# Roots by one activation function, thirteen warm products and earlier LayerNorm steps in a one-core decoder layer

## The chip, the cores and the metric

The kernel runs on one core of one Trainium2 chip. The metric is the device time in microseconds (us) of one launch, the median over the runs. Before the change it is 1084.68 us (three runs, 1083.5 to 1085.56).

## The reference

One layer of a decoder with two groups of heads, on 256 prompt tokens and 8 x 4 sample tokens, 288 columns in all, float32. D_MODEL is 2048, the convolution and pool groups have 1024 channels each, the feed-forward part 8192.

```python
def rmsnorm(x, g):
    return x * lax.rsqrt(jnp.mean(x * x, axis=-1, keepdims=True) + EPS) * g

h = rmsnorm(x, norm1_g)
proj = h @ w_in + b_in
a, gate, z = proj[..., :1024], proj[..., 1024:2048], proj[..., 2048:]
u_ext = concat([hist_conv, a * sigmoid(gate)])
c = silu(layernorm(depthwise_causal_conv(u_ext, conv_w, conv_b), ln_g, ln_b))
z_ext = concat([hist_pool, z])
d = multiscale_pool(z_ext, pos0)            # windows 2, 4, 8, 16
p = group_matmul(d, pool_w) * pool_scale
x = x + concat([c, p]) @ w_out
h2 = rmsnorm(x, norm2_g)
x = x + square(relu(h2 @ w_ff1)) @ w_ff2
y = rmsnorm(x, norm_f)
```

Outputs are y for both groups of tokens and the new histories (the last 30 inputs of the convolution, the last 15 of the pools).

## The kernel before

**Layout.** Channels lie on the 128 partitions and the 288 tokens in the free dimension. A product is a 128x128 block of weights against 128x288 columns, summed in PSUM. To keep float32 precision with fp32r operands, each operand is split into a high part (`hi`, a cast) and a low part (`lo`, the rest), and each product is made of three: hi x hi, lo x hi and hi x lo. In the profile `whi` and `wlo` are weights; `hx`, `dx`, `mx`, `ax` and `fx` are the right-hand sides of w_in, the pools and their part of w_out, the convolution's part of w_out, w_ff1 and w_ff2.

**Stages.** w_in's column pairs come in the order of SEQUENCE: convolution pairs c0 to c7, pools p3 to p0, and the pools' own products P3 to P0. Then w_out runs over the pools' rows (eight groups `g` of two banks, `mixp`), and again over the convolution's rows (`mixc`), while LayerNorm over the convolution's output is done between the products of the first pass. Then come four chunks of w_ff1 and w_ff2, the final norm and the output.

**First products.** x and the first weights come pair by pair of rows, k = 0, 2, ..., 14 (`first_load`). `first_split` (L359) makes their parts: `hi` on ScalarE (L364, L371), the right-hand sides on ScalarE (L369) and for k = 0 on VectorE (L367), the low parts on VectorE (L373, L376). Ahead of them TensorE runs warm products that nothing reads (L213). The first gemm has four banks (pairs c0 and c1) and 24 products for each pair of rows.

**Norms.** The products run on the columns before their norm is known; what comes out is multiplied by the row of inverse roots afterwards. `squares` (L411) sums x squared: ScalarE squares (L418), VectorE adds (L420); a copy from the high weights of k = 4 (L413) holds the squares back until those are there. `rsqrt_sums` (L238) sums over the partitions by products of one column (TensorE), has ScalarE take the square root (L250), then VectorE the reciprocal and a Newton step (L253 to L256). `spread` (L259) brings the result to all partitions by three products with an identity. It serves the first norm (`first_sums`, `first_rows`) and LayerNorm (`ln_sums`, `ln_rows`). The second norm (L638) and the final one (L704 to L712) use ScalarE's Sqrt and `inverse_root` (L231). `load_table` (L207) applies a function to one column, so that its ACT_TABLE_LOAD comes early.

**Order.** A scheduler orders each engine's instructions by readiness and priority; a lower number goes first, and priorities go by the order of the code. `later(by)` (L111) adds `by` to it, a million as a rule; a negative value brings what it encloses ahead of everything else that is ready. `issue_after(ins)` holds an instruction behind another. `chain` keeps TensorE's products in the order of the code until it is cleared ahead of P1. `between` (L338) has a gemm call a step at a given row pair: LayerNorm's mean, sums and rows come in groups 5, 6 and 7 of the first w_out pass (L579). `classes` (L332) puts the first products of a gemm in another order; TURN (L70) has 48 places. Normally the right-hand side alternates between rows 1 and 3 and rows 0 and 2 of its tile.

**Low parts.** WAYS (L73) tells by stage who makes the low part of a block: V is VectorE (L279), G is GpSimd (L282), D is the negated high part by ScalarE (L276) and a DMA from GpSimd's queue that adds the weights to it (L277). There are six raw blocks and five split ones. GpSimd also makes the products of the convolution's history (L464), which wait for `u_all` (L449).

Of the kernel before, what the change touches and what calls it, by code (L numbers as in the profile page):

```python
# [9 lines left out]
F32 = mybir.dt.float32  # L10
# [76 lines left out]
def trunk_kernel(ctx: ExitStack, tc: tile.TileContext, io):  # L87
# [119 lines left out]
    def load_table(func, src):  # L207

        return nc.scalar.activation(few[: src.shape[0], :], src, func)

    load_table(AF.Sqrt, ones[:, 0:1])
    warm = ms("warm")
    for j in range(9):  # L213
        nc.tensor.matmul(warm[:, 0, 0:P], ones, ones, start=True, stop=True)
# [16 lines left out]
    def inverse_root(mean, root, y, out):  # L231

        nc.vector.reciprocal(y, root)
        nc.vector.scalar_tensor_tensor(out=root, in0=mean, scalar=EPS, in1=y, op0=ALU.add, op1=ALU.mult)
        nc.vector.scalar_tensor_tensor(out=root, in0=root, scalar=-0.5, in1=y, op0=ALU.mult, op1=ALU.mult)
        nc.vector.scalar_tensor_tensor(out=out, in0=root, scalar=1.5, in1=y, op0=ALU.add, op1=ALU.mult)

    def rsqrt_sums(parts, scale, after=None):  # L238

        pq = ms("pt")
        pt = pq[:, 0, :]
        for n, t in enumerate(parts):
            for j in range(3):
                last = mm(pt[:TB, j : j + 1], t[:, j * TB : (j + 1) * TB], ones[:, 0:1], start=n + j == 0, stop=n == len(parts) - 1 and j == 2)
        st = const.tile([TB, 12], F32, name=nm("st"))
        s = [st[:, 3 * j : 3 * j + 3] for j in range(4)]
        nc.vector.tensor_scalar(s[0], pt[:TB, 0:3], scale * DC, EPS, op0=ALU.mult, op1=ALU.add)
        nc.scalar.activation(s[1], s[0], AF.Sqrt)  # L250
        if after is not None:
            load_table(after, s[1][:, 0:1])
        nc.vector.reciprocal(s[2], s[1])  # L253
        nc.vector.tensor_tensor(s[3], s[2], s[2], op=ALU.mult)
        nc.vector.scalar_tensor_tensor(out=s[3], in0=s[3], scalar=-0.5, in1=s[0], op0=ALU.mult, op1=ALU.mult)
        nc.vector.scalar_tensor_tensor(out=s[2], in0=s[3], scalar=1.5, in1=s[2], op0=ALU.add, op1=ALU.mult)  # L256
        return s[2], pq[:, 1, :T], last
# [101 lines left out]
    def first_split(k0):  # L359
# [5 lines left out]
        for k in range(k0, k0 + 2):  # L365
            if k == 0:
                nc.vector.tensor_scalar(hx[k][0], xT[:, k, :], v("norm1_g", k), None, op0=ALU.mult)  # L367
# [4 lines left out]
        for b in blocks:  # L372
            nc.vector.tensor_tensor(lo[:, b], raw[:, b], f32(hi[:, b]), op=ALU.subtract)  # L373
# [66 lines left out]
    def conv_pair(i, banks):  # L440
        up = u_all[:, i, 0:UO]
        us = samples(u_all[:, i, UO:UL], US)
        ta, gate = [b[:, :T] for b in banks]
        for b in (gate, ta):
            nc.vector.tensor_tensor(b, b, rb, op=ALU.mult)
        tg = tmpp.tile([P, 2, T], F32, name=nm("tg"), tag="ag", bufs=2)[:, 0, :]
        nc.scalar.activation(tg, gate, AF.Sigmoid, bias=v("b_in", 8 + i))
        for out, a, b in ((up[:, CH:UO], ta[:, :SEQ], tg[:, :SEQ]), (us[:, :, CH:US], samples(ta[:, SEQ:T], NS), samples(tg[:, SEQ:T], NS))):
            nc.vector.scalar_tensor_tensor(out=out, in0=a, scalar=v("b_in", i), in1=b, op0=ALU.add, op1=ALU.mult)  # L449
# [74 lines left out]
    def first_sums():  # L524
        diag.append(rsqrt_sums(squares(), 1.0 / D, AF.Sigmoid))
        return diag[0][2]

    def first_rows():
        pr, last = spread(diag[0])
        nc.scalar.copy(rb, pr)  # L530
# [17 lines left out]
    load_table(AF.Sqrt, f32(mixp[1][0])[:, 0:1])  # L548
# [12 lines left out]
    def ln_sums():  # L561
        ssc = None
        for c in cs:
            nc.vector.tensor_tensor(c, c, norm["mean"][:, None, :].to_broadcast([P, 2, T]), op=ALU.subtract)
# [219 lines left out]
```

## Time and profile before

| | us |
|---|---|
| median of three runs | 1084.68 |
| lowest, highest | 1083.5, 1085.56 |
| the profiled execution | 1084.57 |
| its span, first to last instruction | 1082.8 |
| TensorE busy, of the span | 1071.5 |
| VectorE, ScalarE, GpSimd busy | 635.4, 479.0, 173.6 |
| mean granted TensorE clock | 0.997 of full |

A row of the timeline has start and duration in us, the engine (PE is TensorE's products, PEld its loading of weights, DVE VectorE, ACT ScalarE, POOL GpSimd), the source line, the operation, what is written and read (buffer numbers left out), the shapes and the count of instructions merged in the row. In brackets stands how long the engine was idle before it, and what ended the idle time. A row of the stage windows has the window's borders, its length, and for each engine the busy time and the count; where one engine is asked for, it stands alone, followed by the granted clock, the share of the DMA engines and GB/s. A row of the DMA view ends with the time from issue to landing. Busy times of products overlap, since each begins while the one before drains; the distance of two starts is the step of the stream. A float32 product that is not fp32r counts as two instructions.

### The profile page before, as it was taken

The numbers are of one execution on the slowest core, as the hardware profiler recorded it, in microseconds if no ns is written. First come the engines' busy times: TensorE is split into PE (matmuls) and PEld (weight loads), VectorE is DVE, ScalarE is ACT, GpSimd is POOL, SyncE is SP. The second block draws the span as 40 slices with busy tenths as digits, with TensorE's granted clock in tenths as the row PEclk, the third lists the DMA queues.
The fourth block names the chain that finished last, engine by engine and source line by source line (L and its number), as shares of the span: only waits on it lengthen the run. The fifth ranks groups of instructions, "written<-read, shape, count | busy, mean of one in ns | idle before, by whom it ended". The sixth has DMA issues, their size and how long they took to land.

```text
span 1082.8 us, 19572 instructions
## 1 busy us (share of the span) xinstructions
PE 1071.5 (99%) x8198; PEld 1069.9 (99%) x8198; DVE 635.4 (59%) x818; ACT 479.0 (44%) x585; POOL 173.6 (16%) x180
## 2 busy tenths in 40 slices
PE   9999999999999999999999999999999999999996
PEld 9999999999999999999999999999999999999996
DVE  8899999678655544445544444545544445554553
ACT  8654445475544433334443333444433334444441
POOL 0878979512000000000000000000000000000001
PEclk9999999999999999999999999999999999999998
DMA  9896468545555555555555555555555555555522
GB/s 325 281 273 185 137 196 239 176 152 177 173 164 170 172 166 169 174 164 169 171 168 168 175 165 169 174 167 167 174 165 168 174 169 165 173 166 168 173 78 88
DMA packets 58296, 190.71 MB, mean 176 GB/s; under 512 B 6240, under 2 KB 11232, under 8 KB 58208
## 3 DMA queue, kind: packets, MB, share of 16 engines
q1 hardware_dynamic: 56336, 184.35, 53.9%
q0 software_dynamic: 1008, 3.67, 1.9%
q8 instruction: 64, 1.05, 0.4%
q10 hardware_dynamic: 864, 1.44, 0.4%
q14 instruction: 24, 0.20, 0.1%
HBM read 185.16 MB, written 4.28 MB: 175 GB/s over the span
## 4 chain that ended last, share of the span: by engine, by line
PE 77%; issue 20%; ACT 1%; DVE 0%; DMA 0%; POOL 0%; POOLq 0%
PE ac L305 77%; PE pp L305 1%; DMA wr<-in_w 0%; ACT whi L274 0%; POOL xT L720 0%; ACT n L595 0%; DVE wlo L279 0%; PE pt L305 0%; PE pmean L305 0%; POOLq L770 0%; DVE xT L695 0%; DVE n L592 0%; ACT whi L364 0%; ACT mx L597 0%; DVE hx L367 0%
## 5 line engine op out<-in xcount | busy, mean ns | idle before, releaser
L274 ACT CAST whi<-wr 128x1024 fp32r<-128x1024 f32 (+1 forms) x332 | 348.0, 1049 | 551.4 <-PE ac L305 533.5
L279 DVE TENSOR_TENSOR wlo<-wr,whi 128x1024 fp32r<-128x1024 f32 x288 | 353.1, 1226 | 348.5 <-ACT whi L274 348.5
L305 PE MATMUL ac<-ax,whi 128*128 128x288 f32 x2048 | 351.0, 292 | 0.0
L305 PE MATMUL ac<-fx,whi 128*128 128x288 f32 x2048 | 350.2, 292 | 0.0
L305 PEld LDWEIGHTS ac<-ax,whi 128*128 128x128 f32 x2048 | 296.0, 187 | 0.0
L305 PEld LDWEIGHTS ac<-fx,whi 128*128 128x128 f32 x2048 | 295.6, 187 | 0.0
L305 PE MATMUL ac<-ax,wlo 128*128 128x288 f32 x1024 | 217.4, 292 | 0.0
L305 PE MATMUL ac<-fx,wlo 128*128 128x288 f32 x1024 | 216.4, 292 | 0.0
L305 PEld LDWEIGHTS ac<-ax,wlo 128*128 128x128 f32 x1024 | 162.6, 187 | 0.0
L305 PEld LDWEIGHTS ac<-fx,wlo 128*128 128x128 f32 x1024 | 162.3, 187 | 0.0
L305 PE MATMUL ac<-hx,whi 128*128 128x288 f32 x768 | 131.8, 295 | 1.2 <-DVE hx L367 1.2
L720 POOL TENSOR_TENSOR xT<-xT,rf 128x288 f32<-128x288 f32 x4 | 3.1, 795 | 800.1 <-ACT rf L724 800.1
L305 PEld LDWEIGHTS ac<-hx,whi 128*128 128x128 f32 x768 | 112.1, 190 | 1.4 <-ACT hx L369 1.4
L282 POOL TENSOR_TENSOR wlo<-wr,whi 128x512 fp32r<-128x512 f32 x74 | 100.3, 1410 | 35.3 <-ACT whi L274 34.3
L461 DVE SCALAR_TENSOR_TENSOR pc<-u_all,vec,pc 128x256 f32<-128x256 f32 x232 | 99.5, 483 | 1.9 <-ACT pc L458 0.7
L305 PE MATMUL ac<-hx,wlo 128*128 128x288 f32 x384 | 80.1, 294 | 0.0
L305 PEld LDWEIGHTS ac<-hx,wlo 128*128 128x128 f32 x384 | 61.1, 190 | 0.0
L305 PE MATMUL ac<-dx,whi 128*128 128x288 f32 x256 | 46.0, 296 | 0.0
L305 PE MATMUL ac<-mx,whi 128*128 128x288 f32 x256 | 45.1, 294 | 0.1
L664 DVE SCALAR_TENSOR_TENSOR t<-ac,r 128x576 f32<-128x576 f32 x32 | 24.2, 758 | 25.1 <-PE ac L305 25.1
L305 PEld LDWEIGHTS ac<-dx,whi 128*128 128x128 f32 x256 | 38.0, 188 | 0.2
L305 PEld LDWEIGHTS ac<-mx,whi 128*128 128x128 f32 x256 | 37.5, 188 | 0.6 <-ACT mx L597 0.4
(133 smaller groups left out, 533.6 us busy)
## 6 DMA issues: line engine op xcount, KB each, us to landing
wr<-in_w SPq DMA_DIRECT2D x335, 512.0 KB, 3.8
wlo<-in_w POOLq DMA_DIRECT2D x7, 512.0 KB, 7.7
xT<-in_xT SPq DMA_DIRECT2D x8, 288.0 KB, 7.3
wr<-in_w SPq DMA_DIRECT2D x5, 256.0 KB, 3.6
out_u_out<-u_all SPq DMA_DIRECT2D x1, 1208.0 KB, 9.3
u_all<-in_hist_c SPq DMA_DIRECT2D x8, 136.0 KB, 6.2
out_z_out<-z_all SPq DMA_DIRECT2D x1, 668.0 KB, 9.9
z_all<-in_hist_p SPq DMA_DIRECT2D x4, 152.0 KB, 7.5
```

Source lines behind the costliest of these rows:

```text
L274: nc.scalar.copy(hi, raw)
L279: nc.vector.tensor_tensor(lo, raw, f32(hi), op=ALU.subtract)
L282: nc.gpsimd.tensor_tensor(lo[:, j : j + 2, :], raw[:, j : j + 2, :], f32(hi[:, j : j + 2, :]), op=ALU.subtract)
L305: last = nc.tensor.matmul(*args, **kw)
L461: nc.vector.scalar_tensor_tensor(out=dst, in0=up[:, w : w + SEQ], scalar=cwv[:, w : w + 1], in1=pc, op0=ALU.mult, op1=ALU.add)
L664: nc.vector.scalar_tensor_tensor(out=t, in0=bk[:, :, :T], scalar=0.0, in1=both(rows2[0]), op0=ALU.max, op1=ALU.mult)
L720: eng.tensor_tensor(xk, xk, r[:, None, :].to_broadcast([P, n, T]), op=ALU.mult)
```

## The change

- All four roots use ScalarE's `Abs_reciprocal_sqrt`, which reads the sums in PSUM and adds EPS as its bias. The reciprocal on VectorE is gone, and for the first norm and LayerNorm the operation that scaled the sums too: the scale is in the column that sums them. The Newton step stays, with its intermediate in PSUM. The tables are loaded ahead at the same places.
- 13 warm products for 9.
- In `first_split` the low parts of the first weights are held behind the first right-hand side on VectorE.
- The first norm's steps (squares, sums, rows and the copy `rb`), the gating of the pairs c0 and c1 in `conv_pair` and LayerNorm's sums and rows get a priority ahead of everything else.
- LayerNorm's mean, sums and rows are called one row pair sooner, 12 products each.
- In both passes of w_out the order TURN is in the second group and not the third.
- In making `mixc`, Silu of a pair is held behind the copy of the pair before.

```diff
-        return nc.scalar.activation(few[: src.shape[0], :], src, func)
-    load_table(AF.Sqrt, ones[:, 0:1])
+        return nc.scalar.activation(few[: src.shape[0], :], src, func, bias=ones[: src.shape[0], 0:1], scale=0.0)
+    load_table(AF.Abs_reciprocal_sqrt, ones[:, 0:1])
     warm = ms("warm")
-    for j in range(9):
+    for j in range(13):
...
-    def inverse_root(mean, root, y, out):
-        nc.vector.reciprocal(y, root)
-        nc.vector.scalar_tensor_tensor(out=root, in0=mean, scalar=EPS, in1=y, op0=ALU.add, op1=ALU.mult)
-        nc.vector.scalar_tensor_tensor(out=root, in0=root, scalar=-0.5, in1=y, op0=ALU.mult, op1=ALU.mult)
-        nc.vector.scalar_tensor_tensor(out=out, in0=root, scalar=1.5, in1=y, op0=ALU.add, op1=ALU.mult)
+    def inverse_root(mean, y, t, out, after=None):
+        nc.scalar.activation(y, mean, AF.Abs_reciprocal_sqrt, bias=eps[: y.shape[0], :])
+        if after is not None:
+            load_table(after, y[:, 0:1])
+        nc.vector.scalar_tensor_tensor(out=t, in0=mean, scalar=EPS, in1=y, op0=ALU.add, op1=ALU.mult)
+        nc.vector.scalar_tensor_tensor(out=t, in0=t, scalar=-0.5, in1=y, op0=ALU.mult, op1=ALU.mult)
+        nc.vector.scalar_tensor_tensor(out=out, in0=t, scalar=1.5, in1=y, op0=ALU.add, op1=ALU.mult)
...
-    def rsqrt_sums(parts, scale, after=None):
+    def rsqrt_sums(parts, column, after=None):
         pq = ms("pt")
-        pt = pq[:, 0, :]
+        mean, t = pq[:TB, 0, 0:3], pq[:TB, 0, 4:7]
...
-        s = [st[:, 3 * j : 3 * j + 3] for j in range(4)]
-        nc.vector.tensor_scalar(s[0], pt[:TB, 0:3], scale * DC, EPS, op0=ALU.mult, op1=ALU.add)
-        nc.scalar.activation(s[1], s[0], AF.Sqrt)
...
-        return s[2], pq[:, 1, :T], last
+        inverse_root(mean, st[:, 0:3], t, st[:, 4:7], after=after)
+        return st[:, 4:7], pq[:, 1, :T], last
...
-                nc.vector.tensor_scalar(hx[k][0], xT[:, k, :], v("norm1_g", k), None, op0=ALU.mult)
+                first = nc.vector.tensor_scalar(hx[k][0], xT[:, k, :], v("norm1_g", k), None, op0=ALU.mult)
...
         for b in blocks:
-            nc.vector.tensor_tensor(lo[:, b], raw[:, b], f32(hi[:, b]), op=ALU.subtract)
+            with tc.issue_after(first.ins) if k0 == 0 else nullcontext():
+                nc.vector.tensor_tensor(lo[:, b], raw[:, b], f32(hi[:, b]), op=ALU.subtract)
...
     def conv_pair(i, banks):
+        with later(-LATER if i < 2 else 0):
...
     def first_sums():
-        diag.append(rsqrt_sums(squares(), 1.0 / D, AF.Sigmoid))
+        with later(-LATER):
+            diag.append(rsqrt_sums(squares(), mean_d, AF.Sigmoid))
...
     def first_rows():
-        pr, last = spread(diag[0])
-        nc.scalar.copy(rb, pr)
+        with later(-LATER):
+            pr, last = spread(diag[0])
+            nc.scalar.copy(rb, pr)
...
     def ln_sums():
+        with later(-LATER):
...
     def ln_rows():
-        norm["rows"], last = spread(norm["sums"])
+        with later(-LATER):
+            norm["rows"], last = spread(norm["sums"])
...
-    BETWEEN = {5: {4: ln_mean}, 6: {6: ln_sums}, 7: {2: ln_rows}}
+    BETWEEN = {5: {2: ln_mean}, 6: {4: ln_sums}, 7: {0: ln_rows}}
...
-            last = gemm(each(bk), [mixp[k] for k in korder], between=BETWEEN.get(g, {}), classes=TURN if g == 2 else "")
+            last = gemm(each(bk), [mixp[k] for k in korder], between=BETWEEN.get(g, {}), classes=TURN if g == 1 else "")
...
-            nc.scalar.activation(n[:, m, :], n[:, m, :], AF.Silu, bias=v("ln_b", i), scale=v("ln_g", i))
+            with tc.issue_after(copied) if j else nullcontext():
+                nc.scalar.activation(n[:, m, :], n[:, m, :], AF.Silu, bias=v("ln_b", i), scale=v("ln_g", i))
...
-        nc.scalar.copy(mh, n)
+        copied = nc.scalar.copy(mh, n).ins
...
-        last = gemm(each(bk), mixc, classes=TURN if g == 2 else "")
+        last = gemm(each(bk), mixc, classes=TURN if g == 1 else "")
...
-        nc.scalar.activation(root, mean, AF.Sqrt, bias=eps)
-        inverse_root(mean, root, r2, r2)
+        inverse_root(mean, r2, root, r2)
...
-    nc.scalar.activation(root, sums_f, AF.Sqrt, bias=eps[:TB, :])
-    inverse_root(sums_f, root, first, s_f)
+    s_f = cst[:TB, 6:9]
+    inverse_root(sums_f, cst[:TB, 2:5], ends[:TB, 0, 4:7], s_f)
```

More of the change, by code (lines that the diff above doesn't have):

```diff
@@ L547, in trunk_kernel @@
             pool_products(i)
-    load_table(AF.Sqrt, f32(mixp[1][0])[:, 0:1])
+    load_table(AF.Abs_reciprocal_sqrt, f32(mixp[1][0])[:, 0:1])
     with later(2 * LATER):
@@ L706, in trunk_kernel @@
                 nc.tensor.matmul(idle[:, 0:P], ones, ones, start=True, stop=True)
-    root, first, s_f = [cst[:TB, 2 + 3 * j : 5 + 3 * j] for j in range(3)]
-    nc.scalar.activation(root, sums_f, AF.Sqrt, bias=eps[:TB, :])
-    inverse_root(sums_f, root, first, s_f)
+    s_f = cst[:TB, 6:9]
+    inverse_root(sums_f, cst[:TB, 2:5], ends[:TB, 0, 4:7], s_f)
     for spread_f in (rows_f, again):
```

46 lines of the change are left out of this document (20 added, 26 removed).

## The prediction

> **What bounds the kernel now.** The page first: its first part tells which engine fills the span.
>
> ```profile
> span 1082.8 us, 19572 instructions
> PE 1071.5 (99%) x8198; PEld 1069.9 (99%) x8198; DVE 635.4 (59%) x818; ACT 479.0 (44%) x585; POOL 173.6 (16%) x180
> ```
>
> TensorE is in work 99% of the span, so only three things can move the end: time in which it waits, time in which it steps slowly, and the ends of the span where it has nothing to do. A busy share doesn't show slow steps, so I next read starts of products in the timeline, and one row of the stage windows.
>
> ```profile
> 191.26 0.42 PE L305 MATMUL ac<-dx,wlo 128*128 128x288 f32 x2
> ...
> 192.04 0.42 PE L305 MATMUL ac<-dx,wlo 128*128 128x288 f32 x2
> ...
> 204.78 0.43 PE L305 MATMUL ac<-dx,wlo 128*128 128x288 f32 x2
> ...
> 205.58 0.43 PE L305 MATMUL ac<-dx,wlo 128*128 128x288 f32 x2
> ```
>
> ```profile
> 284.00:1069.00 785.00, 785.00 (x6040) 1.00 0.52 163
> ```
>
> From one low-part pair to the next are six products: 0.78 us in the first two rows (130 ns a product), 0.80 us in the next two (133.3 ns). The row of the windows, TensorE alone, has 6040 products in 785.00 us, 130.0 ns each: the long stage runs on the quick step. The slow step comes up after a break in the stream and stays until the products that TURN has put in another order have passed: in the first w_out pass TURN is at g == 2, and there 0.80 becomes 0.78.
>
> Then the start, where the first real product waits and a second, larger loss stands.
>
> ```profile
> 1.04 4.21 PE L214 MATMUL warm<-ones 128*128 128x128 f32 x18 [1.04 <-DVE cst L229]
> ...
> 5.59 0.54 ACT L369 ACTIVATE hx<-xT,vec 128x288 fp32r<-128x288 f32 x1 [0.35 <-DMA xT<-in_xT]
> ...
> 5.89 0.36 DVE L367 TENSOR_SCALAR hx<-xT,vec 128x288 fp32r<-128x288 f32 x1
> ...
> 6.40 1.30 PE L305 MATMUL ac<-hx,whi 128*128 128x288 f32 x4 [1.15 <-DVE hx L367]
> ...
> 8.45 2.12 PE L305 MATMUL ac<-hx,whi 128*128 128x288 f32 x8
> ...
> 10.84 1.05 ACT L364 CAST whi<-wr 128x1024 fp32r<-128x1024 f32 x1
> ...
> 11.80 0.96 ACT L369 ACTIVATE hx<-xT,vec 128x288 fp32r<-128x288 f32 x2
> ...
> 12.67 0.20 ACT L413 COPY z_all<-whi 128x10 f32<-128x10 f32 x1
> 12.89 2.41 ACT L418 ACTIVATE z_all<-xT 128x576 f32<-128x576 f32 x4
> ...
> 15.21 1.04 ACT L364 CAST whi<-wr 128x1024 fp32r<-128x1024 f32 x1
> ...
> 16.59 1.22 DVE L373 TENSOR_TENSOR wlo<-wr,whi 128x1024 fp32r<-128x1024 f32 x1
> ...
> 16.83 2.27 PE L305 MATMUL ac<-hx,whi 128*128 128x288 f32 x16
> ...
> 18.94 1.21 PE L305 MATMUL ac<-hx,wlo 128*128 128x288 f32 x8
> ```
>
> The nine warm products (18 instructions) end at 5.25; TensorE idles 1.15 us and starts the real work at 6.40 with products 240 ns apart (eight last 2.12 us at 8.45, against 1.21 us at 18.94). About 18 run so before the clock is granted near 10.6: 18 x 110 ns = 2.0 us lost.
>
> **The change, part by part.** The sum is made against the profiled execution: 1084.57 us, its span 1082.8 and 1.8 around it; the median of the runs is 1084.68, so the two may stand for each other.
>
> *Warm products, and the norm's first product ahead of the low parts.* Thirteen are 26 instructions. The grant came 4.2 us after unbroken work began (6.40 to 10.6); unbroken from 1.04 it comes near 5.2, when some 19 have run (0.21 us each); the last 7 at half that end near 6.0. With L367 ahead of L373 on VectorE, L367 can start with L369 at 5.59 and the first product near 6.13, where hx of k = 1 is ready: 0.27 us sooner, and at full step. The low part behind it comes near 6.65, as the fifth product asks for it.
>
> [...]
>
> Without waits this would be worth 0.27 + 2.0 = 2.3 us. But the squares (L413, L418) now have a million steps of priority, and ScalarE does them as soon as the cast that gates them is done at 11.89 (10.84 + 1.05). Ahead of hx and the cast of rows k = 6, 7 then stand 0.20 + 2.41: hx ends at 11.89 + 2.61 + 0.96 = 15.46, the cast at 16.50, the low part (1.22) at 17.75. TensorE, with 72 products of three pairs at 130 ns, is there at 6.13 + 9.4 = 15.5 and waits about 1.0 us. Before, it used this cast at 16.83 + 8 x 0.13 = 17.87 (I take the first 8 of those 16 as the pair before) and the low part at 18.94. So 1.2 us is left; I take 1.15. Later pairs cost ScalarE 2.7 us each (a square 0.6, hx 0.96, cast 1.04), TensorE 3.1: no further wait. The wait falls on the 73rd product, inside the first TURN (the 37th to the 84th): should that leave the slow step until the next one, some 126 products later, 0.4 is lost. Bounds: 0.4 (that, or a square's addition and a leftover of hx ahead of the low part), 2.3 if the squares don't come first.
>
> *Roots.* The two steps over three columns (first norm, LayerNorm) go from five VectorE operations to three, the other two from four to three; ScalarE reads PSUM itself.
>
> ```profile
> 32.47 0.59 PE L305 MATMUL pt<-ones,z_all 128*96 128x1 f32 x6
> ...
> 33.28 0.21 ACT L250 ACTIVATE st<-st 96x3 f32<-96x3 f32 x1 [1.44 <-DVE st L249]
> ...
> 35.52 0.16 DVE L256 SCALAR_TENSOR_TENSOR st<-st 96x3 f32<-96x3 f32 x1
> 35.74 0.74 PEld L305 LDWEIGHTS pt<-ident,st 96*128 96x128 f32 x6 [0.17 <-DVE st L256]
> ...
> 1071.27 0.26 ACT L708 ACTIVATE cst<-ends,cst 96x3 f32<-96x3 f32 x1 [0.19 <-PE ends L703]
> 1071.57 0.17 DVE L233 RECIPROCAL cst<-cst 96x3 f32<-96x3 f32 x1 [1.53 <-ACT cst L708]
> 1071.85 0.16 DVE L234 SCALAR_TENSOR_TENSOR cst<-ends,cst 96x3 f32<-96x3 f32 x1
> ...
> 1072.45 0.91 PE L712 MATMUL ends<-ident,cst 96*128 96x96 f32 x6 [0.21 <-DVE cst L236]
> ```
>
> First norm: from 33.06 to 35.68 the step took 2.6 us; one ScalarE operation (0.26 at L708) and three of 0.16 with their gaps make some 1.1, so the 0.17 us that the spread product waited goes: I take 0.1. Tail: everything from 1071.27 to 1072.45 sets the end, and L233 leaves with the gap behind it (1071.57 to 1071.85): 0.25 us, 0.1 to 0.3 should the PSUM target of the next three cost. The second norm's reciprocal is hidden under a running stream. ACT_TABLE_LOADs: as many as before, if the new function's table holds Square and Copy as Sqrt's does; the trace can't show that.
>
> *LayerNorm 12 products sooner.* All three steps and what they issue (4 + 6 + 6 TensorE instructions, VectorE's and ScalarE's; no DMA) move together, 12 x 0.133 = 1.6 us.
>
> ```profile
> 195.80 0.48 DVE L461 SCALAR_TENSOR_TENSOR c<-u_all,vec,pc 128x256 f32<-128x256 f32 x1
> ...
> 201.15 0.65 PE L305 MATMUL pmean<-sum_c,ones 128*128 128x288 f32 x2
> ...
> 208.94 0.46 DVE L571 TENSOR_TENSOR q<-q 128x288 f32<-128x288 f32 x1
> ...
> 210.11 0.59 PE L305 MATMUL pt<-ones,q 128*96 128x1 f32 x6
> ...
> 219.00 0.43 PE L305 MATMUL ac<-dx,whi 128*128 128x288 f32 x2
> ...
> 219.55 0.54 PE L305 MATMUL ac<-mx,whi 128*128 128x288 f32 x2
> ...
> 221.59 0.42 PE L305 MATMUL ac<-mx,wlo 128*128 128x288 f32 x2
> ```
>
> The mean's input is done at 196.28, 4.9 us ahead of its use: moving by 1.6, and TensorE's own 1.2 at the start, leaves 2. The sums end 0.7 us ahead of 210.11, with equal distance to the mean as before, and with priority. At the far end 14 products start between 219.00 and 221.59, 2.59 us where 1.87 are due: 0.72 us of waiting for mx, which 1.6 us more room covers. The new order of Silu and copy gives the first pair of mx sooner still. I take 0.72; bounds 0 and 0.8.
>
> *TURN one group sooner, twice.* 48 products each at 130 instead of 133.3: 2 x 0.16 = 0.32; bounds 0 and 0.4.
>
> *Priorities for the first two convolution pairs.* Nothing for TensorE by themselves; they decide the first rival.
>
> Sum: 1.15 + 0.1 + 0.25 + 0.72 + 0.32 = 2.54; **1084.57 - 2.54 = 1082.0 us.**
>
> **Rivals.** *(1) A low part by DMA gives the start's gain back.* In convolution 3 GpSimd issues an accumulating DMA behind two products of the history.
>
> ```profile
> 40.56 4.33 POOL L464 TENSOR_TENSOR prd<-u_all,vec 128x992 f32<-128x992 f32 x2 [0.94 <-DVE u_all L449]
> ...
> 44.83 1.06 POOL L277 DMA_DIRECT2D wlo<-in_w  x1
> ...
> 50.91 0.42 PE L305 MATMUL ac<-hx,wlo 128*128 128x288 f32 x2
> ```
>
> ```profile
> wlo<-in_w POOLq DMA_DIRECT2D x1, 512.0 KB, 5.8
> ```
>
> By the DMA view's row of that issue it lands at 44.83 + 5.8 = 50.6, and TensorE wants it at 50.91: 0.3 us to spare. TensorE 1.25 us sooner waits 0.95 unless the issue moves. The priorities speak for a move (u_all is ready some 2 us sooner, L464 starts in GpSimd's idle 0.94); a static order that puts L464 elsewhere speaks against. With the wait comes the slow step up to TURN at i == 5, some 250 x 3.3 ns = 0.8: 1082.0 + 1.8 = 1083.8.
>
> *(2) The squares don't delay the cast:* 2.3 in place of 1.15: 1080.9.
>
> *(3) The w_out groups are interleaved again.* Now the first group's sum (L609) comes 12.3 us behind the first mx product at 219.55, the time of two groups.
>
> ```profile
> 231.87 0.76 DVE L609 TENSOR_TENSOR xT<-xT,ac 128x576 f32<-128x576 f32 x1 [2.40 <-PE ac L305]
> ```
>
> Then TURN, now in the second, is scattered, and the slow step lasts from the second group to the TURN at L657: 7 x 48 + 96 products x 3.3 ns = 1.4: 1082.0 + 1.4 = 1083.4. For it: mx of the later pairs is still made at ScalarE's pace between casts. Against: 48 instead of 36 products of room.
>
> *(4) Slower: the long stage takes the slow step.* One TURN stands ahead of it (L657), behind the second norm's two products, whose surroundings are now scheduled anew. Should it end on the wrong step, 785 us x (133.3/130 - 1) = 20.1: 1102. It decides from 190 us on the slow step (4.7 us, the gain and 0.2% more). Against it: TURN ended on 0.78 in the first w_out pass, and on 130.0 ns ahead of the 785 us.
>
> **How the numbers follow.** Forecast 0.54, rivals 0.12, 0.12, 0.08 and 0.14. The forecast's own range is 1081.2 to 1083.0, from the bounds of its terms. 0.2%, about what a measurement tells here from no change, is 2.2 us: 1082.5 and 1086.8. About 0.40 of the forecast's 0.54 and all of rival 2 lie under the first: faster 0.52. Rival 4 alone is over the second: 0.14. The rest is 0.34. From 1080.7 to 1084.2 lies all but rival 4 and a few hundredths.
>
> **What would show it.** Right: 26 warm instructions, TensorE at full step from 6.1, a wait of 1 us near 15.5 to 16.5, no wait ahead of the first mx product, 0.78 per six products from the second w_out group on, no reciprocal in the tail. Wrong: a wait near 50, more ACT_TABLE_LOADs than before, any stretch over 200 us at 0.80 per six, or products 240 ns apart behind 8 us.

## The result, and the profile after

The changed kernel takes 1088.66 us, the median of six runs (1087.17 to 1089.93), against 1084.77 of the kernel before (six runs too); the ratio is 1.0035 (95%: 1.0025 to 1.0045). It is slower by 3.9 us where a gain of 2.5 us was forecast. Its profiled execution took 1087.26 us with a span of 1085.2, so 2.4 us of the loss stand in the traces; where the other 1.4 are is answered further down. Lines of the changed kernel are numbered a little lower: L305 has become L299, L570 L569, L571 L570, L464 L460, L277 L271, L282 L276, L279 L273, L274 L268.

The head of the changed kernel's page, then its timeline (start, duration, engine, line, what is written and read) at the start and the first norm:

```profile
span 1085.2 us, 19581 instructions
PE 1073.4 (99%) x8206; PEld 1071.9 (99%) x8206; DVE 631.9 (58%) x812; ACT 478.1 (44%) x585; POOL 173.9 (16%) x180
```

```profile
1.04 5.23 PE L214 MATMUL warm<-ones 128*128 128x128 f32 x26 [1.04 <-DVE cst L229]
...
6.15 0.77 PE L299 MATMUL ac<-hx,whi 128*128 128x288 f32 x4
...
14.84 1.03 ACT L358 CAST whi<-wr 128x1024 fp32r<-128x1024 f32 x1
...
16.23 1.22 DVE L368 TENSOR_TENSOR wlo<-wr,whi 128x1024 fp32r<-128x1024 f32 x1
...
17.50 1.33 PE L299 MATMUL ac<-hx,wlo 128*128 128x288 f32 x8 [0.23 <-DVE wlo L368]
...
31.47 0.59 PE L299 MATMUL pt<-cst,z_all 128*96 128x1 f32 x6
```

The start came as forecast: 26 warm instructions, real products from 6.15 with no cold ones, and short stalls at the operands of k = 6 between 15.9 and 17.7, 0.84 us together. The first norm's sums, at 32.47 before, start at 31.47, one microsecond sooner.

That microsecond is gone 20 us later. The third convolution pair's part by DMA, in the timeline and in the DMA view (last number: us from issue to landing):

```profile
39.66 4.33 POOL L460 TENSOR_TENSOR prd<-u_all,vec 128x992 f32<-128x992 f32 x2 [1.09 <-DVE u_all L445]
...
43.93 1.06 POOL L271 DMA_DIRECT2D wlo<-in_w  x1
...
49.20 0.68 PE L299 MATMUL ac<-hx,whi 128*128 128x288 f32 x4
49.94 0.53 PE L299 MATMUL ac<-hx,wlo 128*128 128x288 f32 x2
```

```profile
wlo<-in_w POOLq DMA_DIRECT2D x1, 512.0 KB, 6.0
```

It was issued 0.90 us sooner than before and landed at 49.93; TensorE, 1.2 us sooner than before, wanted it at 49.72 (four products at 0.13 from 49.20) and started at 49.94. The stall is 0.22 us, but the slow step comes with it. The windows of TensorE (length, busy time, number of products, clock, DMA share, GB/s), first of the kernel before, then of the changed one:

```profile
53.00:81.00 28.00, 28.00 (x218) 1.00 0.97 271
...
236.00:284.00 48.00, 48.00 (x371) 1.00 0.58 179
```

```profile
53.00:81.00 28.00, 28.00 (x212) 1.00 0.96 267
...
236.00:284.00 48.00, 48.00 (x362) 1.00 0.53 172
284.00:1069.00 785.00, 785.00 (x6039) 1.00 0.51 164
```

Six products fewer from 53 to 81 us are 0.8 us. The second pair of windows lies in the second w_out pass: nine fewer, 1.2 us. The long stage runs at 130 ns as before. Then LayerNorm, in the changed kernel's timeline:

```profile
200.00 0.65 PE L299 MATMUL pmean<-sum_c,ones 128*128 128x288 f32 x2
...
201.17 2.75 DVE L563 TENSOR_TENSOR c<-c,pmean 128x576 f32<-128x576 f32 x4 [1.81 <-PE pmean L299]
...
202.89 1.05 ACT L268 CAST whi<-wr 128x1024 fp32r<-128x1024 f32 x1 [0.24 <-PE ac L299]
203.85 1.25 ACT L565 ACTIVATE q<-c 128x576 f32<-128x576 f32 x2
204.02 1.29 POOL L276 TENSOR_TENSOR wlo<-wr,whi 128x512 fp32r<-128x512 f32 x1 [1.76 <-ACT whi L268]
204.56 1.37 DVE L569 TENSOR_TENSOR q<-q,q 128x576 f32<-128x576 f32 x1 [0.64 <-ACT q L565]
205.26 1.82 POOL L276 TENSOR_TENSOR wlo<-wr,whi 128x512 fp32r<-128x512 f32 x1
206.03 1.67 DVE L569 TENSOR_TENSOR q<-q,q 128x576 f32<-128x576 f32 x1
...
208.69 0.43 PE L299 MATMUL ac<-dx,whi 128*128 128x288 f32 x2
...
210.09 0.45 DVE L570 TENSOR_TENSOR q<-q 128x288 f32<-128x288 f32 x1
...
210.68 0.64 PE L299 MATMUL pt<-ones,q 128*96 128x1 f32 x6 [1.56 <-DVE q L570]
```

The products ahead of the sums start at 208.69 and 208.82, so the sums were due at 208.95; they start at 210.68, 1.7 us late, because their operand is ready only at 210.54. From the mean to that point the work took 10.5 us (200.00 to 210.54), before 8.25 (201.15 to 209.40). The grouped instructions of 203 to 210 us tell which part grew, before and after (mean ns ahead of the second bar):

```profile
L570 DVE TENSOR_TENSOR q<-q,q 128x576 f32<-128x576 f32 x3 | 2.3, 764 | 0.0
```

```profile
L569 DVE TENSOR_TENSOR q<-q,q 128x576 f32<-128x576 f32 x3 | 3.8, 1260 | 0.7 <-ACT q L565 0.6
```

The three additions of squares took 1.5 us more, and the first waited 0.6 us for a square, since a weight cast (202.89) had come between the first and second square. The two long additions (204.56 to 207.70) lie where GpSimd makes the two halves of a low part (204.02 to 207.08). Before, these came under the subtractions and had ended by 205.16; in the timeline of the kernel before:

```profile
202.31 2.75 DVE L564 TENSOR_TENSOR c<-c,pmean 128x576 f32<-128x576 f32 x4 [3.33 <-PE pmean L305]
202.60 2.56 POOL L282 TENSOR_TENSOR wlo<-wr,whi 128x512 fp32r<-128x512 f32 x2 [0.63 <-ACT whi L274]
```

At the far end, the second norm's first product and the tail:

```profile
286.98 0.43 PE L299 MATMUL mean<-hl,means 128*128 128x288 f32 x2
...
1072.01 0.59 PE L703 MATMUL ends<-cst,ssf 128*96 128x1 f32 x6
...
1074.81 0.91 PE L711 MATMUL ends<-ident,cst 96*128 96x96 f32 x6
```

The same three products of the kernel before:

```profile
284.35 0.42 PE L305 MATMUL mean<-hl,means 128*128 128x288 f32 x2
...
1069.38 0.59 PE L703 MATMUL ends<-cst,ssf 128*96 128x1 f32 x6
...
1072.45 0.91 PE L712 MATMUL ends<-ident,cst 96*128 96x96 f32 x6 [0.21 <-DVE cst L236]
```

The second norm stands 2.63 us later than before, the tail's first sums too, the last spread 2.36. Comparing the start of the same product in both traces gives the whole account; a minus is sooner than before. Products are counted as TensorE's instructions of the kernel before, its 18 warm ones included, and the times are that kernel's.

| up to | difference, us | what happened in between |
|---|---|---|
| the first norm's sums | -1.0 | no cold products |
| product 306, 46 us | -1.2 | no wait for the first norm's rows |
| product 690, 96 us | 0.0 | stall and slow step behind the third pair's part by DMA |
| product 1506, 203 us | +0.45 | TURN in the second w_out group leaves the slow step |
| product 1602, 216 us | +2.15 | the wait ahead of LayerNorm's sums |
| product 1650, 223 us | +1.47 | no wait for mx |
| the second norm | +2.63 | TURN in the second group of the second pass leaves the slow step |
| the last spread | +2.36 | shorter root in the tail |

### The profile page after: what moved, and what is told of

Its sections match the earlier page's. It is cut to its first block, busy times and chain, and to the rows that moved or that the text cites. A ratio compares the mean times of both kernels' runs of the same rounds, so it can differ in the third digit from the quotient of the medians.

```text
span 1085.2 us, 19581 instructions
## 1 busy us (share of the span) xinstructions
PE 1073.4 (99%) x8206; PEld 1071.9 (99%) x8206; DVE 631.9 (58%) x812; ACT 478.1 (44%) x585; POOL 173.9 (16%) x180
## 3 DMA queue, kind: packets, MB, share of 16 engines
q10 hardware_dynamic: 864, 1.44, 0.4%
## 4 chain that ended last, share of the span: by engine, by line
PE 74%; issue 21%; DMA 2%; ACT 1%; DVE 1%; POOL 1%; SPq 0%; POOLq 0%; ACTq 0%; DVEq 0%
PE ac L299 73%; DMA wr<-in_w 1%; PE pp L299 1%; DMA wlo<-in_w 1%; ACT z_all L413 0%; ACT hx L363 0%; ACT whi L358 0%; DVE q L569 0%; POOL prd L460 0%; POOL wlo L276 0%; POOL xT L719 0%; SPq L191 0%; PE pt L299 0%; DVE wlo L368 0%; ACT whi L268 0%
## 5 line engine op out<-in xcount | busy, mean ns | idle before, releaser
L268 ACT CAST whi<-wr 128x1024 fp32r<-128x1024 f32 (+1 forms) x332 | 347.1, 1046 | 557.2 <-PE ac L299 539.2
L273 DVE TENSOR_TENSOR wlo<-wr,whi 128x1024 fp32r<-128x1024 f32 x288 | 353.1, 1226 | 353.2 <-ACT whi L268 353.2
L299 PE MATMUL ac<-ax,whi 128*128 128x288 f32 x2048 | 351.2, 292 | 0.0
L299 PE MATMUL ac<-fx,whi 128*128 128x288 f32 x2048 | 350.1, 292 | 0.0
L299 PEld LDWEIGHTS ac<-ax,whi 128*128 128x128 f32 x2048 | 296.2, 187 | 0.0
L299 PEld LDWEIGHTS ac<-fx,whi 128*128 128x128 f32 x2048 | 295.6, 187 | 0.0
L299 PE MATMUL ac<-ax,wlo 128*128 128x288 f32 x1024 | 217.4, 292 | 0.0
L299 PE MATMUL ac<-fx,wlo 128*128 128x288 f32 x1024 | 216.3, 292 | 0.0
L299 PEld LDWEIGHTS ac<-ax,wlo 128*128 128x128 f32 x1024 | 162.7, 187 | 0.0
L299 PEld LDWEIGHTS ac<-fx,wlo 128*128 128x128 f32 x1024 | 162.2, 187 | 0.0
L299 PE MATMUL ac<-hx,whi 128*128 128x288 f32 x768 | 131.3, 294 | 0.1
L299 PEld LDWEIGHTS ac<-hx,whi 128*128 128x128 f32 x768 | 111.5, 188 | 0.3 <-ACT whi L358 0.3
L276 POOL TENSOR_TENSOR wlo<-wr,whi 128x512 fp32r<-128x512 f32 x74 | 101.3, 1427 | 36.6 <-ACT whi L268 34.0
L299 PE MATMUL ac<-hx,wlo 128*128 128x288 f32 x384 | 80.1, 294 | 0.3 <-DVE wlo L368 0.2
L299 PEld LDWEIGHTS ac<-hx,wlo 128*128 128x128 f32 x384 | 60.6, 188 | 0.8 <-DVE wlo L368 0.5
L299 PE MATMUL ac<-dx,whi 128*128 128x288 f32 x256 | 46.3, 297 | 0.0
L299 PE MATMUL ac<-mx,whi 128*128 128x288 f32 x256 | 45.3, 296 | 0.0
L299 PEld LDWEIGHTS ac<-dx,whi 128*128 128x128 f32 x256 | 38.2, 189 | 0.2
L299 PEld LDWEIGHTS ac<-mx,whi 128*128 128x128 f32 x256 | 38.0, 189 | 0.0
```

What stands on the lines that cost most here:

```text
L268: nc.scalar.copy(hi, raw)
L273: nc.vector.tensor_tensor(lo, raw, f32(hi), op=ALU.subtract)
L276: nc.gpsimd.tensor_tensor(lo[:, j : j + 2, :], raw[:, j : j + 2, :], f32(hi[:, j : j + 2, :]), op=ALU.subtract)
L299: last = nc.tensor.matmul(*args, **kw)
```

## The experiments

All ratios are to the kernel before, run on the same chip, with the 95% interval. Experiments ran on four chips, on which the median of the kernel before was 1084.43 to 1084.81 us, so times of two experiments on different chips compare to some 0.4 us.

**The changed kernel again**, with nothing edited.

> The changed kernel once more, for a second profile: its profiled execution was 1087.26 us while the median of its runs is 1088.66. Theory (the losses are fixed by the order of instructions): the wait ahead of LayerNorm's sums (1.7 us), the wait at convolution 3's low part (0.2 to 0.4 us) and the slow step (0.80 us per six products) up to about 85 us and from 162 to 288 us are there again, to 0.3 us. Rival (they come and go from run to run): at least one of them is missing or differs by over 0.5 us, and a slower execution shows a stretch of slow step that the first profile hasn't.

1088.57 us, 1.0033 (1.0023 to 1.0043). The wait ahead of the sums is there again (210.71), and the lead is gone at 110 us, though TensorE waited only 0.03 us for the third pair's part by DMA this time; the slow step came all the same. So the loss repeats.

**LayerNorm at its old places.**

```diff
-    BETWEEN = {5: {2: ln_mean}, 6: {4: ln_sums}, 7: {0: ln_rows}}
+    BETWEEN = {5: {4: ln_mean}, 6: {6: ln_sums}, 7: {2: ln_rows}}
```

> LayerNorm's mean, sums and rows back at their old row pairs, the rest as changed. Theory (the place decides what runs beside the sums): the two long additions of squares (1.36 and 1.66 us) are back at about 0.75 to 0.8, the wait ahead of the sums (1.7 us) is gone, and the 0.7 us wait ahead of the first mx product is back: 0.8 to 1.0 us less than the changed kernel by 220 us. Rival (the roots or priorities make the chain longer): the wait ahead of the sums stays over 1 us, and the run is some 0.7 us slower than the changed kernel.

1085.82 us, 1.0008 (0.9999 to 1.0017); no wait ahead of the sums, and the additions of squares are back at 0.75 to 0.80 us. The move costs 2.8 us in the median, a microsecond more than the wait in the profile. The wait for mx stays away here too, without the move that was to remove it.

**TURN in the third group**, both passes.

```diff
-... classes=TURN if g == 1 else "")
+... classes=TURN if g == 2 else "")
```

> TURN in the third group again in both passes of w_out, the rest as changed. Theory (in the second group it is mixed with the end of the first group's products and doesn't bring back the quick step): 0.78 us per six products from about 190 us to LayerNorm and from about 235 us on; 0.3 us less before LayerNorm and 1.2 us less between 235 and 288 us, together 1.5 us less than the changed kernel. Rival (the step has another cause, such as the wait at LayerNorm's sums): 0.80 per six stays to 288 us, and the run is within 0.3 us of the changed kernel.

1087.1 us, 1.0022 (1.0013 to 1.0031), 1.5 less. Apart from the wait ahead of the sums and what follows it, this trace loses nothing to the slow step from 100 us to the second norm. TensorE's program order has the first two groups of each pass interleaved, before and after. The order of high and low weight parts in the traces shows it: in the kernel before and in this one TURN's 48 products stand in one piece, in the changed kernel products of another group stand among them, about 12 in the first pass and 24 in the second. Mixed so, they don't restore the quick step: 362 products from 236 to 284 us in the changed kernel, 371 in this one and in the kernel before.

The profile of this kernel caught something else. Behind the wait, in its timeline and windows:

```profile
211.73 0.64 PE L299 MATMUL pt<-ones,q 128*96 128x1 f32 x6 [1.56 <-DVE q L570]
...
212.85 1.12 PE L299 MATMUL ac<-dx,whi 128*128 128x288 f32 x4
213.77 0.69 PE L299 MATMUL ac<-dx,wlo 128*128 128x288 f32 x2
214.25 1.17 PE L299 MATMUL ac<-dx,whi 128*128 128x288 f32 x4
```

```profile
213.00:216.00 3.00, 3.00 (x15) 0.50 0.72 257
```

From 213 us products start 240 ns apart at a granted clock of 0.50: two starts at 213.77 and the next at 214.25. Thirteen such products cost 13 x 0.11 = 1.4 us.

**No part by DMA in the third pair** (VectorE makes it).

```diff
-WAYS = {... "c3": "GDGG", ...}
+WAYS = {... "c3": "GVGG", ...}
```

> In convolution 3 the low part that an accumulating DMA made is made by VectorE, the rest as changed. Theory (that DMA's landing gives back the start's gain): no wait near 49.6 us, 0.78 us per six products from 50 to 83 us, TensorE 1.1 to 1.2 us ahead of the kernel before at 90 us in place of 0.03, and the run 1.1 us less than the changed kernel. Rival (the next accumulating DMA, of convolution 4 or pool 3, each with 0.3 to 0.9 us to spare before, takes its place): a wait near 62, 68 or 75 us and the slow step from there to 85, and less than 0.6 us of the 1.1 is kept.

1088.54 us, 1.0033 (1.002 to 1.0045): nothing in the median. The stall and the slow step from 50 us are gone (at 105 us TensorE is 0.08 us ahead of the kernel before, where at the first norm's sums it was 0.11 behind), but in this execution the first weights came late, the first norm's sums started at 32.58 instead of 31.47, and there was no lead to keep. The clock hides a part, too: the mean granted clock was 0.995 or 0.996 in five of its six executions and in 8 of the changed kernel's 15 (more on this below), and among these the medians are 1088.77 and 1089.37. Alone it decides nothing; on top of the next kernels it does.

**The move alone, in the kernel before.**

```diff
-    BETWEEN = {5: {4: ln_mean}, 6: {6: ln_sums}, 7: {2: ln_rows}}
+    BETWEEN = {5: {2: ln_mean}, 6: {4: ln_sums}, 7: {0: ln_rows}}
```

> The kernel before with LayerNorm's three steps 12 products sooner and nothing else. Theory (the place alone makes the loss): TensorE waits 1.4 to 1.9 us ahead of the sums near 209 us, because two of the additions of squares fall under GpSimd's low parts and take 1.3 us and more in place of 0.75; the median is 1086 to 1088 us. Rival (the wait needs the changed kernel's other edits, the shorter root chain or the order of the SiLUs): no wait above 0.3 us ahead of the sums and 1084.2 to 1085.2 us.

1086.84 us, 1.0017 (1.0008 to 1.0026). The wait is the same to a hundredth:

```profile
209.22 0.64 PE L305 MATMUL pt<-ones,q 128*96 128x1 f32 x6 [1.56 <-DVE q L571]
```

The place alone makes the wait; roots and priorities have no part in it.

This trace also tells of the start, which here is that of the kernel before, with nine warm products. TensorE waited 1.2 us for its first operand, as in the kernel before, and the first norm's sums began as soon as with thirteen:

```profile
31.33 0.59 PE L305 MATMUL pt<-ones,z_all 128*96 128x1 f32 x6
```

From a first product near 6.4 us, that is 135 ns on average for the 184 products ahead of them, against 142 in the kernel before and 138 in the changed one. So the cold products up to 10.6 us, from which the forecast took its first term, belong to some executions of the kernel before and not to all.

**Warm products alone, in the kernel before.**

```diff
-    for j in range(9):
+    for j in range(13):
```

> The kernel before with 13 warm products in place of 9 and nothing else. Theory (the start's gain is given back at the first part by DMA of the third conv pair): TensorE is 0.5 to 2 us ahead of the kernel before at product 114, waits at product 320 to 350 or runs on the slow step from there to 83 us, and is level within 0.3 us at product 690; median 1084.4 to 1085.2 us. Rival (a start's gain goes through to the end when the other edits are gone): 1083.3 to 1084.1 us.

1084.07 us, 0.9996 (0.9987 to 1.0005), not told apart from no change. In its trace the first norm's sums come at 31.38, 1.1 us ahead; the slow step from 62 to 82 us takes half of it, and 0.5 us stays. Both sides get something: the lead isn't lost whole, but it doesn't go through. Against the theory, the third pair's part by DMA takes nothing. It is issued 1.1 us sooner than in the kernel before, without any priority, and lands at 49.45; TensorE uses it at 49.82 without a wait:

```profile
43.75 1.02 POOL L277 DMA_DIRECT2D wlo<-in_w  x1
...
49.82 0.42 PE L305 MATMUL ac<-hx,wlo 128*128 128x288 f32 x2
```

```profile
wlo<-in_w POOLq DMA_DIRECT2D x1, 512.0 KB, 5.7
```

**Old places and third group together.** LayerNorm as in the second experiment, TURN as in the third.

> The changed kernel with LayerNorm's three steps in the old places and the balancing orders in the third group of both projections, as before; roots, warm products and priorities stay. Theory (the two moves make the whole loss; they add up: 2.8 us and 1.6 us): 1083.9 to 1084.7 us, no wait ahead of the sums, the slow step ends at about 178 and 232 us as before. Rival (one of them only shows through the other, so that with both undone the time stays at that of the old places alone): 1085.3 to 1086.2 us.

1084.05 us, 0.9992 (0.9984 to 1.0001). The two moves are the whole loss, and they add up: 1088.66 to 1085.82 to 1084.05. Its window of the second pass has the count of the kernel before:

```profile
236.00:284.00 48.00, 48.00 (x371) 1.00 0.56 179
```

**The same, and no part by DMA in the third pair.**

> The kernel of the run before this one in the list, with the one low part by DMA of the third conv pair made by VectorE. Theory (that part's landing takes back the start's gain): no wait at products 306 to 354, quick step until 160 us, and the start's lead of 0.3 to 1.2 us kept at product 690: 1082.9 to 1084.0 us. Rival (VectorE's extra low part delays something else by as much, or the lead is lost at a later part by DMA): the same as the run before it in the list, or more.

1083.36 us, 0.9986 (0.9977 to 0.9995): faster than both kernels, 1.2 us under the one before and 5.3 under the changed one. There is no stall near 50 us; the next part by DMA, the fourth pair's, is now the one that stalls, by 0.27 us (due at 62.52, four products from 62.00):

```profile
62.00 0.68 PE L299 MATMUL ac<-hx,whi 128*128 128x288 f32 x4
62.79 0.54 PE L299 MATMUL ac<-hx,wlo 128*128 128x288 f32 x2
```

**That part made by VectorE too.**

```diff
-WAYS = {... "c4": "GDGD", ...}
+WAYS = {... "c4": "GVGD", ...}
```

> The kernel with old places, third group and no part by DMA in the third conv pair, and with the first of the fourth pair's two parts by DMA made by VectorE too. Theory (the start's lead is lost at whichever part by DMA comes next): no wait near 62 us, quick step until 160 us, and 0.3 to 0.6 us less than without this edit: 1082.7 to 1083.1 us. Rival (VectorE or a later part by DMA takes its place): 1083.2 us or more.

1085.05 us, 1.0004 (0.9995 to 1.0013). Slower than without this edit, as the rival had it, though the theory is half right: TensorE keeps its lead of 0.8 us unchanged from product 306 to product 690 on the quick step. But VectorE, with one more low part, is late in the pool stage:

```profile
159.57 0.53 PE L299 MATMUL pp<-dx,whi 128*128 128x288 f32 x2 [0.41 <-ACT dx L498]
...
165.74 0.54 PE L299 MATMUL ac<-dx,wlo 128*128 128x288 f32 x2 [0.57 <-DVE wlo L273]
...
169.94 0.53 PE L299 MATMUL pp<-dx,whi 128*128 128x288 f32 x2 [0.49 <-DVE dx L511]
```

**TURN of the first products behind the wait for k = 6**, on top of that kernel.

```diff
-... classes="01" * 18 + TURN, by_part=True)
+... classes="01" * 42 + TURN, by_part=True)
```

> The kernel of the run before this one in the list, with the balancing order of the first products 48 products later, behind the waits for the operands of k=6 and 7 that leave TensorE on the slow step from 19 to 29 us. Theory (the order balances what is ahead of it, so it has to come after the last wait): no slow step between 24 and 48 us, 0.3 us less than without this edit: 1082.4 to 1082.8 us. Rival (the order's own place does not matter): the same time within 0.15 us, slow step from 19 to 29 us.

1084.87 us, 1.0007 (0.9998 to 1.0016), 0.18 less. The theory's own sign failed: from 25 us to the first norm's sums the slow step is there with this edit too (the last 13 products ahead of the sums at 31.52 take 1.73 us, 133 ns each). The trace lost 0.2 us between 66 and 114 products where the kernel without the edit lost 0.9, but its first product came 0.6 us later, so less was left to wait for. What this TURN's place is worth stays open.

**Products in the wait.** Four more products of constants ahead of LayerNorm's sums in the changed kernel; their result is not used.

```diff
+        for j in range(fill):
+            mm(pq[:, 1, 0:P], ones, ones, start=True, stop=True)
```

> The changed kernel with four more 128x128 products of the constant ones (about 1.7 us of TensorE's time) directly ahead of LayerNorm's sums, so that TensorE works through most of the 1.7 us in which it waits for them; their result is not used. Theory (in about half of the executions the idle 1.7 us also lower the granted clock for some 3 us): the granted clock is 0.997 or 0.998 in nearly all executions, none of the profile's products run at 240 ns for 3 us, and the median falls from 1088.6 to 1086.8 to 1087.7 us, the level of the changed kernel's undisturbed executions. Rival (the clock drops for another reason): granted clocks of 0.995 in about half of the executions as in the changed kernel, and 1088.2 to 1089 us.

1087.64 us, 1.003 (1.0019 to 1.0042). The scheduler put them some 3 us ahead of the sums instead of directly before; the wait behind them is 0.76 us. In all six executions the mean granted clock was 0.997 or 0.998. In the changed kernel's 15 executions of both runs it was 0.998 in seven, with times of 1087.0 to 1088.5, and 0.995 or 0.996 in eight, with 1088.6 to 1090.4. The medians of these two groups are 2.0 us apart, and the median of all lies between them; so the 1.4 us between median and profiled execution are put down to the clock, lowered behind the 1.7 us wait in about half of the executions.

**Any order of the SiLUs**, on top of the kernel with old places and third group: the order behind `copied` is taken out.

> The kernel with LayerNorm's old places and the balancing orders in the third group, without the order that puts the SiLUs of each pair behind the cast of the pair before. Theory (the shorter root chain takes away the 0.7 us wait for the first mx operand near 218 us): that wait stays below 0.2 us and the time is 1083.8 to 1084.4 us. Rival (the order of the SiLUs does it): the wait of 0.5 to 0.8 us is back and the time is 1084.5 to 1085.0 us.

1084.32 us, 0.9998 (0.9989 to 1.0007). By the time it lies between the two theories; the trace is clearer. A wait of 0.4 us stands again between mx products (the next is due at 220.01), and over the stage TensorE gains nothing on the kernel before where it gains 0.7 us with the order:

```profile
219.75 0.42 PE L299 MATMUL ac<-mx,wlo 128*128 128x288 f32 x2
...
220.40 0.53 PE L299 MATMUL ac<-mx,whi 128*128 128x288 f32 x2 [0.23 <-DVE xT L587]
```

At the old places the shorter roots don't remove the wait for mx; the order of the SiLUs does.

**The last low part of the first pass by VectorE**, in the changed kernel, so that GpSimd has nothing under the additions.

```diff
-"w0": "VV", "w": "GG"
+"w0": "VV", "w7": "GV", "w": "GG"
```

> The changed kernel with the last low part of the first projection made by VectorE in place of GpSimd, so that no work of GpSimd lies under LayerNorm's additions of squares. Theory (GpSimd's work on the same operands' side slows the additions): all three additions take 0.75 to 0.80 us, where two took 1.36 and 1.66 us; VectorE's own low part of 1.21 us stands ahead of them, so the wait ahead of the sums only falls, from 1.7 to between 0.3 and 1.2 us. Rival (the additions are slow by themselves at that place, by their operands or by the casts beside them): one or two of them still take over 1.2 us.

1086.46 us, 1.0015 (1.0005 to 1.0024). The additions (min, median, max in ns; first the changed kernel, then this one):

```profile
L569 DVE TENSOR_TENSOR q<-q,q x3: 746/1369/1666, 204.6 to 208.3; 128x576 f32<-128x576 f32 x3
```

```profile
L569 DVE TENSOR_TENSOR q<-q,q x3: 748/749/753, 205.0 to 208.3; 128x576 f32<-128x576 f32 x3
...
209.68 0.64 PE L299 MATMUL pt<-ones,q 128*96 128x1 f32 x6 [0.70 <-DVE q L570]
```

All three are back at 0.75 us with no work of GpSimd beside them, and the wait fell to 0.86 us (due 208.82), although VectorE has 1.2 us more to do. Its ten executions all had a clock of 0.997 or 0.998.

**The mean another 12 products sooner**, in the changed kernel.

```diff
-    BETWEEN = {5: {2: ln_mean}, 6: {4: ln_sums}, 7: {0: ln_rows}}
+    BETWEEN = {5: {0: ln_mean}, 6: {4: ln_sums}, 7: {0: ln_rows}}
```

> The changed kernel with LayerNorm's mean another 12 products sooner, the sums and rows where the change has them, so that 72 products in place of 60 lie between mean and sums (9.6 in place of 8.0 us). Theory (the step that fails is the distance from mean to sums, which the chain of 9.8 us needs): the wait ahead of the sums is below 0.4 us, no products at 240 ns behind it, and the time 1.5 to 2.8 us below the changed kernel's: 1085.8 to 1087.1 us. Rival (the chain grows with its place, since another cast, addition or low part slips in): the wait stays above 1 us and the time above 1087.5 us.

1085.41 us, 1.0009 (0.9999 to 1.0018), 3.2 under the changed kernel, more than expected. No wait ahead of the sums. One addition is still long, and the last one of half a tile takes 1.44 us, both under GpSimd's low parts of 204.34 to 207.40; but the distance now has room for them. Sums placed 12 products sooner are possible; they need the mean 24 products sooner.

## Why the prediction was wrong

**Start: right in this pair of traces, in part by luck, and given back.** The sum's 1.15 us was 1.0 at the first norm. The grant of the full clock came near 5.4 us, where 5.2 was forecast. But the term was taken from an execution whose cold products lasted to 10.6 us, and with the move alone, whose start is the old one, the sums came at 31.33 as well.

Rival 1, given 0.12, then took the whole microsecond, but not for the reason it gives. It let the lead eat the 0.3 us to spare unless the issue moves, and asked the priorities for the move. The issue moves with the start by itself: from issue to first use are 6.08 us in the kernel before, 6.07 with thirteen warm products alone and 6.08 with the move alone, which were 1.1 us ahead and didn't wait. In the nine traces with the changed roots and this part by DMA the distance is 5.65 to 5.79 us, with TensorE early or late: with TURN in the third group it was 0.3 us later than in the kernel before and waited 0.22 us all the same. So 0.29 us of the margin of 0.31 went; 0.19 of it is the removed wait for the first norm's rows, which brings the use nearer, and 0.10 the issue, later behind the sums by a cause that stays open. With 5.7 us from issue to landing with thirteen warm products alone, 5.8 in the kernel before, 6.0 in the changed one and 6.1 with old places and third group, the part then lands just in time or too late by chance of the execution. In eight of the nine the slow step begins there (212 products from 53 to 81 us in the changed kernel, 218 in the kernel before). Stall and slow step cost 1.2 us.

**Roots: right.** The wait for the first norm's rows is gone, worth 0.2 (0.1 forecast), and the tail gives 0.27 (2.80 us from 1072.01 to 1074.81 against 3.07 from 1069.38 to 1072.45) for 0.25. What the first of them costs at the third pair's part by DMA, the prediction didn't see.

**LayerNorm: the step that failed.** "The sums end 0.7 us ahead of 210.11, with equal distance to the mean as before, and with priority" took the chain's length as fixed and moved it. The chain grew from 8.25 to 10.5 us with its place, by the additions under GpSimd's low parts (1.5 us) and a cast between two squares (0.7): 1.7 us of waiting, and in half of the executions the clock. The priority didn't help: with the move alone, which has none, ScalarE, VectorE and GpSimd work in the same order up to the sums. In the changed kernel's trace it was the cast that wasn't ready: the second of the four subtractions had ended at 202.59, ScalarE was free from 202.64, and the cast ahead of the second square began at 202.89, when a product had ended. Why the scheduler put it ahead in spite of the priority stays open. The forecast looked at the ends of the moved steps and not at what lies beside them at the new place.

The traces show which of VectorE's work grew beside GpSimd's. The additions, which take two SBUF tiles, went from 0.75 to 1.37 and 1.67 us beside the low parts, while the subtractions from the mean, whose second input is in PSUM, took 2.75 us for four in the kernel before, almost wholly beside a low part (202.60 to 205.16), and the same 2.75 us in the changed one, beside a low part only up to 202.26. The rows show that the additions and the halves of the low part took turns: the first addition ended 0.62 us behind the first half (205.31 to 205.93), the second half took 1.82 us in place of 1.29 and ended 1.15 behind that addition, and the second addition ended 0.62 behind that half (207.08 to 207.70). Each that came while the other worked seems to have waited for its end.

**The wait for mx: right in size, but the move wasn't needed.** It went, 0.68 of 0.72 us, but at the old places too. There the order of the SiLUs, which the prediction mentions as a help and prices at nothing, does it. With the move alone, which has no such order, the mx products don't wait either; as the lowered clock left 1.4 us more room in that trace, it doesn't show whether the move would have sufficed.

**TURN one group sooner: wrong sign.** 0.32 of gain was forecast, 0.45 + 1.16 = 1.6 us were lost. The step assumed that TURN restores the quick step wherever it stands; in these traces it did so in the third group and not in the second, which is interleaved with the one before (371 and 362 products from 236 to 284 us). Rival 3 saw this for the second pass (1.4 us) at a chance of 0.08; the first pass it didn't consider, though there too the groups are interleaved.

**Priorities: about nothing, as forecast**, as far as the runs tell, for none takes them out alone, and rival 4 did not come: 6039 products in the 785 us.

The terms so far give 1.0 + 0.2 - 1.2 - 0.45 - 1.7 + 0.7 - 1.16 + 0.27 = -2.3, the loss of the profiled execution's span to a tenth; the clock adds the rest of the median.

## What to carry to other kernels

A chain that is moved under a running stream must be priced again at the new place, with what each of its engines and their neighbours do there; its old length, here 8.25 us, held only for its old neighbours (10.5 at the new place). The transfer that is issued behind the same start moved with it (6.07 us from issue to first use with a lead of 1.1 us, 6.08 without), so a lead alone needn't use up its margin; what does is anything that shortens the way from its issue to its first use, here 0.29 of 0.31 us. So list these distances, with the scatter of the landing, before adding up gains. The order of products that balances this stream did so in a group that nothing else was mixed into (371 products from 236 to 284 us) and not in one mixed with another (362); that it need only stand behind the last disturbance wasn't borne out.

## What the runs showed of the hardware

A wait of 1.7 us in a stream that had run for 200 us lowered the granted clock to 0.50 for some 3 us, beginning 0.8 to 1.4 us behind its end, in three of the five traces that have it: with TURN in the third group (0.50 from 213 to 216 us), without the third pair's part by DMA (products 240 ns apart from 211.35 to 214.71) and with the move alone (from 210.6 to 213.97). By the mean granted clock it did so in 8 of 15 executions of the changed kernel, 5 of 10 with TURN in the third group and 5 of 6 without the third pair's part by DMA; waits of 0.76 and 0.86 us did so in none of 6 and 10. (With the move alone the mean was as low in 7 of 11, but on that chip also in 8 of 33 of the kernel before, so not all seven need come from the wait.) What decides in which executions the clock drops wasn't shown.

The start itself differs between executions: hx and weights for k = 2 were there without a wait in some (in the changed kernel's trace the first 72 products started 133 ns apart, up to 15.57), and the first norm's sums came anywhere from 31.38 to 32.94 us in kernels with the same 13 warm products, and at 31.33 and 32.47 in two with nine. Single profiles can't resolve a start's gain of 0.5 us.
